# A last strip of 7 KB of each row instead of 6 KB, to release the first store sooner

## Chip, cores and metric

The kernel runs on one core of a Trainium2 chip. The metric is the device time of one execution in microseconds (us).

## The reference

```python
def setup_inputs():
    batch, c, h, w = 32, 3, 256, 256
    return {"x": np.random.randn(batch, c, h, w).astype(np.float32)}

def reference(x):
    return np.rot90(x, k=2, axes=(-2, -1)).astype(np.float32)
```

Each of the 96 images of 256 x 256 is turned by 180 degrees, that is, its 65,536 numbers are put in reverse order. 25.17 MB are read and 25.17 MB written.

## The kernel before

The input is cut into three tiles, A, Bt and Ct, each of 128 partitions with 64 KB (16,384 floats). VectorE reverses each row of a tile in place through a small tile T; the store writes the four rows of an image in reverse order. All transfers are issued by SyncE.

```python
    def load(t, g, lo, hi):
        return nc.sync.dma_start(out=t[:, lo:hi], in_=x4[g][:, lo:hi])

    def store(t, g):
        return nc.sync.dma_start(out=o4[g][:, ::-1, :], in_=t[:, :])
    # ... inside(t): 12 copies on VectorE that reverse a tile in place
    TAIL = 1536
    load(A, 0, 0, E)
    load(Bt, 1, 0, E)
    body = load(Ct, 2, 0, E - TAIL)
    load(Ct, 2, E - TAIL, E)
    inside(A)
    first = store(A, 0)
    tc.add_manual_dep(
        first.ins, body.ins.name,
        mybir.DependencyInfo(mybir.DependencyClass.Sync, mybir.DependencyReason.DATA),
        reason="the first store is queued while the last strip is on its way")
    for g, t in ((1, Bt), (2, Ct)):
        inside(t)
        store(t, g)
```

The third load is in two pieces, a body and a strip of `TAIL` columns. The first store doesn't need either; it is made to wait until the body has landed, and is issued while the strip is still on its way.

## Time and profile before

| | |
|---|---|
| median of 3 runs | 122.15 us (122.03 to 122.24) |
| DMA queue's share of 16 engines | 97.3% |
| VectorE busy | 37% |
| first store issued | 59.48 us |

The span of the profile (120.2 us) is shorter than the time: the rest lies outside the core's program. One more source is used below: the trace records the start and duration of every DMA packet. Every transfer shows 128 data packets, a row or a piece of a row in each, and 16 packets of 9 ns that count up the semaphore, one for each DMA engine; that is 8 rows and one semaphore packet for an engine. The records don't name the engine, so "the last strip end" is the latest end of such a packet over the 16 engines, "the mean strip end" their mean, and the same for the store's first packets. The "mean gap" is the mean start of the store's first packets less the mean strip end; the "bubble" is this idle time between strip and store. The "skew" is how far the last of the 16 semaphore packets of a transfer is behind their mean.

### The profile page before, as it was taken

To read this page: it belongs to the slowest core of one execution; us is meant where nothing else is said; L and a number is where in the kernel's file an instruction comes from. 1 tells how busy PE (TensorE), PEld (TensorE's weight loads), DVE (VectorE), ACT (ScalarE), POOL (GpSimd) and SP (SyncE) were. 2 spreads that over 40 slices of the span, in tenths; PEclk is the share of its full clock that TensorE was granted. 3 is DMA by queue.
4 is the path that set the end of the run, shared out by engine and by line. 5 is a ranking of instruction groups with operands and counts; after the bars stand their busy time and mean duration, and the time that the engine had idled before them with its cause. 6 is when DMAs were issued, how large, how long until landed. Compare 5 with 4: busy or idle time off the path is not lost.

```text
span 120.2 us, 93 instructions
## 1 busy us (share of the span) xinstructions
DVE 44.2 (37%) x36; POOL 0.2 (0%) x4
## 2 busy tenths in 40 slices
DVE  0000000499995099999059999400000000000000
POOL 0000000000000000000000000000000000000000
DMA  9888988898889779779499888988898889888990
GB/s 349 349 349 371 676 349 349 371 676 349 349 349 698 316 316 632 316 336 613 202 408 698 349 349 349 698 349 349 349 698 349 349 349 698 349 349 349 632 414 0
DMA packets 1008, 50.33 MB, mean 419 GB/s; under 512 B 112, under 2 KB 112, under 8 KB 240
## 3 DMA queue, kind: packets, MB, share of 16 engines
q1 hardware_dynamic: 1008, 50.33, 97.3%
HBM read 25.17 MB, written 25.17 MB: 419 GB/s over the span
## 4 chain that ended last, share of the span: by engine, by line
DMA 34%; DVE 25%; another core or an unknown queue 4%; issue 1%; SPq 0%; DVEq 0%
DMA Bt<-in_x_dram 34%; DVE T L52 8%; DVE Bt L52 8%; DVE Ct L52 8%; SPq L55 0%; DVEq L52 0%
## 5 line engine op out<-in xcount | busy, mean ns | idle before, releaser
L52 DVE COPY T<-A 128x2048 f32<-128x2048 f32 x4 | 4.9, 1227 | 22.6 <-DMA A<-in_x_dram 22.5
L52 DVE COPY T<-Ct 128x2048 f32<-128x2048 f32 x4 | 4.9, 1227 | 4.5 <-DMA Ct<-in_x_dram 4.4
L52 DVE COPY T<-Bt 128x2048 f32<-128x2048 f32 x4 | 4.9, 1227 | 4.4 <-DMA Bt<-in_x_dram 4.3
L52 DVE COPY Bt<-T 128x2048 f32<-128x2048 f32 x4 | 4.9, 1227 | 0.1
L52 DVE COPY A<-T 128x2048 f32<-128x2048 f32 x4 | 4.9, 1227 | 0.1
L52 DVE COPY Ct<-T 128x2048 f32<-128x2048 f32 x4 | 4.9, 1227 | 0.1
L52 DVE COPY A<-A 128x2048 f32<-128x2048 f32 x4 | 4.9, 1227 | 0.1
L52 DVE COPY Bt<-Bt 128x2048 f32<-128x2048 f32 x4 | 4.9, 1227 | 0.1
L52 DVE COPY Ct<-Ct 128x2048 f32<-128x2048 f32 x4 | 4.9, 1226 | 0.1
L95 POOL MEMSET const-uint8-127<- 128x1 uint8 x1 | 0.1, 102 | 0.0
L95 POOL MEMSET const-bfloat16-1.0<- 128x1 bf16 x1 | 0.1, 101 | 0.0
L95 POOL MEMSET const-float32-0.0<- 128x1 f32 x1 | 0.1, 98 | 0.2 <-issue 0.2
L95 POOL MEMSET const-float32-1.0<- 128x1 f32 x1 | 0.1, 98 | 0.0
## 6 DMA issues: line engine op xcount, KB each, us to landing
Ct<-in_x_dram SPq DMA_DIRECT2D x1, 7424.0 KB, 57.7
Ct<-in_x_dram SPq DMA_DIRECT2D x1, 768.0 KB, 59.2
A<-in_x_dram SPq DMA_DIRECT2D x1, 21.8
Bt<-in_x_dram SPq DMA_DIRECT2D x1, 40.7
out_dram<-A SPq DMA_DIRECT2D x1, 21.3
out_dram<-Bt SPq DMA_DIRECT2D x1, 39.9
out_dram<-Ct SPq DMA_DIRECT2D x1, 42.9
```

Source lines behind the costliest of these rows:

```text
L52: tc.keep_in_program_order(nc.vector.tensor_copy(out=dst, in_=src))
L95: nc = _bacc.Bacc("TRN2", target_bir_lowering=False, num_devices=1)
```

## The change

The intent is to let the first store be queued a little sooner, so that no DMA engine runs dry between the last load and the first store.

```diff
-    TAIL = 1536
+    TAIL = 1792
     load(A, 0, 0, E)
     load(Bt, 1, 0, E)
     body = load(Ct, 2, 0, E - TAIL)
```

## The prediction

> **What bounds the kernel now.** I read the page first: how busy each engine is, and what the DMA queue took.
>
> ```profile
> span 120.2 us, 93 instructions
> DVE 44.2 (37%) x36; POOL 0.2 (0%) x4
> ...
> q1 hardware_dynamic: 1008, 50.33, 97.3%
> HBM read 25.17 MB, written 25.17 MB: 419 GB/s over the span
> ```
>
> VectorE is busy for 37% of the span, the 16 DMA engines for 97.3%. All seven transfers are on one queue, so the kernel is one long row of packets per DMA engine: 24 rows of 64 KB in, 24 rows out. The reader should see how little is left: 2.7% of 120.2 us is 3.2 us, and the start (1.8 us before the first packet) and the end (1.1 us after the last one) hold 2.9 us of it. What lies between is some 0.3 us at most, and the change can only win part of that.
>
> Next the timeline and the waits of the DMA-issuing queue, to see what releases the stores.
>
> ```profile
> 1.64 1.01 SPq L55 DMA_DIRECT2D Ct<-in_x_dram  x2
> ...
> 36.39 1.23 DVE L52 COPY A<-T 128x2048 f32<-128x2048 f32 x1
> ...
> 59.48 0.63 SPq L58 DMA_DIRECT2D out_dram<-A  x1
> 60.20 0.55 SPq L58 DMA_DIRECT2D out_dram<-Bt  x1
> ...
> 76.51 0.54 SPq L58 DMA_DIRECT2D out_dram<-Ct  x1
> ```
>
> ```profile
> SPq L58 <- DMA Ct<-in_x_dram: 57.3, 2, 56.7
> ```
>
> A has been rotated since 37.6 us, but its store is issued only at 59.48, when the body of the third load has landed (its last semaphore increment is at 59.38): that is the added dependency. Only then does SyncE spend 0.63 us on the issue. The second store follows at 60.20, and the third at 76.51; the engines reach the second at about 80.2 and the third at about 99.5 (the packets with the stores' semaphore increments), so these two are never late, the third by 23 us.
>
> The page's chain of waits doesn't help here. It ends at VectorE's last copy (76.5 us) and calls 4.2 us "another core or an unknown queue": that is the landing of the third load. The end of the kernel is the end of the packets, so I looked at the packets alone, in the DMA view of the one microsecond from 60.10 to 61.10, in 40 slices of 25 ns, each packet counted where it starts:
>
> ```profile
> GB/s 737 737 737 246 246 492 246 246 246 492 737 246 246 246 737 0 492 246 0 0 492 0 0 0 0 0 7865 5243 7864 7865 2621 2621 5243 2621 0 0 0 0 0 0
> DMA packets 64, 1.25 MB, mean 1245 GB/s; under 512 B 16, under 2 KB 16, under 8 KB 48
> ```
>
> A 6 KB packet of the strip in a slice is 246 GB/s, a 64 KB packet of the store 2621. So the last two strip packets start in slice 20 (60.60 to 60.63), no packet starts in slices 21 to 25, and the 16 first store packets, one for each DMA engine, start in slices 26 to 33 (60.75 to 60.95). The packet records give the times behind it:
> - the strip's semaphore packets, the last on each engine: from 60.33 to 60.84 us, mean 60.644; each takes 9 ns;
> - the store's first packets: from 60.76 to 60.94 us, mean 60.833.
>
> The mean gap is 60.833 - 60.653 = 0.18 us on each engine. The records don't name the engine, but this mean needs no pairing. Between the first and second load the first packet follows within 10 ns of the semaphore packet (21.593, then 21.599): a full queue has no gap. So the 0.18 us is a bubble that the late release leaves.
>
> **What the Trainium skill says.** "DMA: Bandwidth & Descriptors", section "Queues, rings and completion order": on each engine, descriptors are consumed in ring order, on a ring that all DMAs of one issuing sequencer share. The trace agrees: semaphore packets of the seven transfers come in order of issue. So a store that is queued early waits behind the strip and doesn't overtake it. The same page, section "Why a DMA increments its semaphore by 16 and not by 1": only the full 16 means that all has landed. So the release is set by the body's slowest engine (its semaphore packet is at 58.99 us, its landing 0.39 later), while most engines finish earlier. The same page, "Latency and other measured facts", gives HWDGE about 600 ns to the first byte; here the first store packet starts 60.76 - (59.48 + 0.63) = 0.65 us after the issue ends, so it agrees. Its section "Where 436 GB/s comes from" puts the ceiling of this path at 435 GB/s; 65,536 B in 2.418 us, the usual packet here, are 27.1 GB/s on each engine and 434 on 16. No packet can be hoped to become quicker.
>
> **The change, part by part.** It removes nothing and adds nothing: the same seven transfers, copies and packets. The instruction order differs only in the shapes of the two pieces of the third load (14,848 and 1,536 columns become 14,592 and 1,792).
>
> Cost of the packets: a body packet of 59,392 B follows the next after 2.188 us and a strip packet of 6,144 B after 0.231, together 2.419, as a whole row of 64 KB takes (2.414 to 2.418). The fixed part is about 4 ns a packet. A row cut at 58,368 and 7,168 B is again two packets, so the strip ends where it ends now: cost 0.00 us.
>
> Move of the release: each engine carries 8 rows of the strip. Another 1,024 B of each is 8,192 B, at 27.1 GB/s 0.302 us. The body lands 0.30 us sooner, at about 59.08; the first store is issued at about 59.18 and could start its packets at 60.46 to 60.64 instead of 60.76 to 60.94.
>
> What of it reaches the end: an engine can start the store only when its strip is done, between 60.34 and 60.85. From its slowest body engine to its first store packet the release takes 60.762 - 58.991 = 1.77 us, to the last one 1.95; the strip now covers 8 x 0.231 = 1.85 of it, then 2.15. So the bubble closes on nearly all engines, and the strip becomes what they wait for. The mean start moves by 0.17 to 0.18 us. But the kernel ends with its last engine. The latest store start is 60.944 now and can't come before 60.851, the end of the last strip: 0.093 us. The three latest starts (60.900, 60.905, 60.944) against the three latest strip ends (60.771, 60.842, 60.851) give 0.13, 0.06 and 0.09. From there to the end an engine has 24 packets of 2.42 us whatever happens (the last semaphore packet, 119.104, is 58.16 after the latest start). So I expect 0.09 us from the bubble. To this may come 0.06 us: the store's first packets take 2.48 us, later ones 2.42; if that is the cost of starting an idle engine, it goes too. I count half: 0.03. Sum: about 0.12 us, 0.1% of 122.15, so 122.03.
>
> **The rivals.**
> - The whole 0.30 us reaches the end, which would be 121.85. For it: the release is moved by just that. Against it: the strip can't be hurried, and 0.18 is the mean gap.
> - Nothing reaches the end, 122.15. For it: the engine that ends last may be one whose gap is already nearly nil (the latest start and the latest strip end leave 0.09 at most if they belong to one engine; another engine may decide). The runs of the kernel before lie 0.21 us apart, so this looks the same as my own case in three runs.
> - Reads and writes run together and disturb each other, as the store starts on the quick engines while the slow ones still read their strips: up to 0.4 us of mixing instead of 0.08. If packets became 10% longer in that stretch, it would cost 0.04 us; 122.1. Against it: first store packets start at 60.76 already with strip packets running, and are 3% long.
> - The strip is held up by store packets that go ahead of it, and the third tile lands later. Harmless up to 23 us, as worked out above; the time stays at 122.0 to 122.15.
> - Longer body rows were better for the queue than shorter ones: excluded by the packet times above.
>
> **The range and the chances.** Every way above ends between 121.85 and 122.2; the scatter of the kernel before is 122.03 to 122.24. I predict 122.03 us, 8 in 10 between 121.82 and 122.23. A gain of 2% would be 2.4 us, eight times what all idle time between first and last packet amounts to; a loss of 2% would need a mechanism that nothing in the profile hints at. Faster by over 2%: 0.005. Within 2%: 0.985. Slower by over 2%: 0.01.
>
> **What would show it right or wrong.** In the changed profile: the first store issued at 59.1 to 59.25 instead of 59.48 (the release); its first packets starting between 60.45 and 60.86, more spread than now, with no empty stretch between strip and store (the bubble); the strip's semaphore packets still at 60.33 to 60.84 (no cost of the cut); VectorE's first copy of the third tile still near 61.4; the last packet at about 119.0 instead of 119.1. I am wrong if the store's first packets still start as one group later than the last strip packet, if strip or store packets get longer than 0.27 and 2.5 us, or if the end moves by over 0.3 us either way.

## The result, and the profile after

The changed kernel took 122.31 us (median of 6 runs, 122.04 to 122.44), the kernel before 122.20 us in 6 runs (122.03 to 122.77), 3 of them taken beside those of the changed kernel. The ratio is 0.9997, with a 95% interval from 0.9973 to 1.0021: no difference is seen. The predicted ratio was 0.999, inside the interval. As a time, 122.31 lies 0.08 us above the upper end of the predicted range.

The page of the changed kernel:

```profile
span 120.7 us, 93 instructions
DVE 44.2 (37%) x36; POOL 0.2 (0%) x4
...
q1 hardware_dynamic: 1008, 50.33, 97.2%
```

and its timeline around the release (start, duration, engine, instruction, and what ended the engine's wait):

```profile
59.63 0.63 SPq L58 DMA_DIRECT2D out_dram<-A  x1
60.36 0.55 SPq L58 DMA_DIRECT2D out_dram<-Bt  x1
61.82 1.23 DVE L52 COPY T<-Ct 128x2048 f32<-128x2048 f32 x1 [4.71 <-DMA Ct<-in_x_dram]
```

The first store is issued at 59.63 us, later than the 59.48 of before, though the body is shorter. This profiled run is the slowest of the six (122.44). The DMA view from 60.10 to 61.10 us in slices of 25 ns, as it was shown of before (a strip packet is now 287 GB/s, a store packet still 2621):

```profile
GB/s 573 287 573 860 287 287 860 573 0 0 287 573 287 860 860 0 0 860 287 0 0 0 574 0 287 287 0 0 287 0 0 0 10772 5243 5243 3195 2621 2621 2621 287
DMA packets 62, 1.06 MB, mean 1059 GB/s; under 512 B 12, under 2 KB 12, under 8 KB 50
```

Strip packets still start in slices 22 to 39 (the 287 in the last slice is one), and only 12 of the 16 semaphore packets are in the window: four engines are late. So the packet records, averaged over the 16 engines, say more:

| | before | after |
|---|---|---|
| body: semaphore packets, mean and last | 58.79, 58.99 | 58.70, 59.20 |
| strip end, mean and last | 60.65, 60.85 | 60.86, 61.36 |
| first store packets, first and last | 60.76, 60.94 | 60.91, 61.39 |
| mean gap from strip to store | 0.18 | 0.19 |
| last store start to last semaphore packet | 58.16 | 58.15 |

The mean engine did end its body sooner, but the slowest engine was 0.51 us behind the mean, against 0.20 before, and the release waits for the slowest. Seven body packets that started between 43 and 49 us took 2.26 to 2.46 us where 2.15 is usual, long before the release. The kernel before has such packets too: in its second profile (see below) four were over 5% long, up to 2.36 us where 2.19 is usual. So nothing says that the shorter body rows are at fault. So one profile of each kernel could not answer the question. It took a second profile of both, and larger steps of the same change.

### The profile page after: what moved, and what is told of

Same layout as the page of the kernel before. It is cut to its first block, busy times and chain, and to the rows that moved or that the text cites. A ratio compares the mean times of both kernels' runs of the same rounds, so it can differ in the third digit from the quotient of the medians.

```text
span 120.7 us, 93 instructions
## 1 busy us (share of the span) xinstructions
DVE 44.2 (37%) x36; POOL 0.2 (0%) x4
## 4 chain that ended last, share of the span: by engine, by line
DMA 34%; DVE 25%; another core or an unknown queue 4%; issue 1%; SPq 0%; DVEq 0%
DMA Bt<-in_x_dram 34%; DVE T L52 8%; DVE Bt L52 8%; DVE Ct L52 8%; SPq L55 0%; DVEq L52 0%
```

## The experiments

I began with the theory of the prediction (the "bubble" theory): the kernel ends when the slowest DMA engine's strip is done, plus what of the release's latency the strip doesn't cover, plus 58.16 us. Its rivals: the release is hidden by something else (A), reads and writes that overlap cost time (B), all time by which the release moves reaches the end (C). All ran on one chip.

### Shorter strips: 2 KB and 4 KB

```diff
-    TAIL = 1536
+    TAIL = 512      # e1_strip2k; 1024 in e2_strip4k
```

> Strip of 2 KB a row (512 columns) instead of 6 KB. My theory: the end is the strip end of the slowest DMA engine, plus whatever of the release's latency (1.77 to 1.95 us from the body's last semaphore packet to the store's first packets) the strip does not cover, plus 58.16 us of stores. The strip now covers 8 x 0.080 = 0.64 us instead of 1.85, so the bubble grows by 1.21 us on the slowest engine and the time by about 1.2 us, to 123.4 (ratio 1.010); the mean gap between strip and store rises from 0.18 to about 1.4 us. Rival A, the release is hidden anyway by something else: no change (122.2). Rival B, reads and writes that overlap cost time: less overlap, so less than the 1.2 us.

> Strip of 4 KB a row (1024 columns). My theory: the strip covers 8 x 0.155 = 1.24 us instead of 1.85, so the time rises by 0.60 us to about 122.8 (ratio 1.005), mean gap about 0.8 us. Rival A: 122.2. A straight line through 2, 4 and 6 KB with 0.30 us for each KB is what my theory says; the line must bend at 6 to 7 KB.

Measured: 2 KB: 122.71 us, ratio 1.0036 (1.0021 to 1.0051). 4 KB: 123.00 us, ratio 1.0063 (1.0048 to 1.0078), close to the expected 1.005. But the shorter strip being the quicker of the two fits no theory. The timeline of SyncE in the 2 KB run shows why:

```profile
57.22 0.63 SPq L58 DMA_DIRECT2D out_dram<-Bt  x1
61.31 0.55 SPq L58 DMA_DIRECT2D out_dram<-A  x1
77.18 0.54 SPq L58 DMA_DIRECT2D out_dram<-Ct  x1
```

The scheduler had put Bt's store first, which waits for no part of the third load. With 4 KB the mean gap was -0.003 us (with 2 KB the semaphore packets of body and strip overlap in time and can't be told apart, but a store packet starts within 10 ns of a semaphore packet there too). So there was no bubble to test, and a different loss: the strip's packets ran long, 12 of 128 by over 5% with 2 KB and 39 with 4 KB. These two runs say nothing about the bubble, and the near hit of 4 KB was luck.

### The 2 KB strip in the right order

```diff
-    TAIL = 1536
+    TAIL = 512
...
-        store(t, g)
+        last = store(t, g)
+        if g == 1:
+            tc.add_manual_dep(
+                last.ins, first.ins.name,
+                mybir.DependencyInfo(mybir.DependencyClass.NoSync, mybir.DependencyReason.DATA),
+                reason="the second store is queued after the first")
```

> The 2 KB strip again, now with the first store kept ahead of the second on the queue (in the two runs before, with 2 and 4 KB, the scheduler had put the second store first, so that a store was queued 2.7 to 3.5 us before the strip's end, and they did not test the bubble). Theory of the bubble: nothing is queued before the body has landed, strip 0.64 us, so the bubble grows by 1.21 us on the slowest engine, ratio 1.008 to 1.011, mean gap about 1.4 us, and no strip packet longer than 0.1 us. If the release is hidden: ratio 1.000.

Measured: 123.41 us, ratio 1.0096 (1.0079 to 1.0113), 1.17 us more (0.96% of 122.26) against the 1.21 worked out. The mean gap was 1.45 us, the last store start came 1.20 us after the last strip end instead of 0.08 to 0.09, and no strip packet took over 0.084. In the DMA view from 60 to 63 us (slices of 75 ns) the bubble can be seen as the zeros between strip and store:

```profile
GB/s 82 219 328 328 410 410 437 355 301 273 164 55 27 27 27 0 0 0 0 0 0 0 0 0 0 0 0 0 0 6117 6117 1748 0 0 0 0 0 0 0 0
```

So where the strip is too short, the missing cover does reach the end, nearly one to one. Rival A falls.

### Longer strips, or no dependency

```diff
-    TAIL = 1536
+    TAIL = 4096     # e3_strip16k
```
```diff
-    first = store(A, 0)
-    tc.add_manual_dep(first.ins, body.ins.name, ...)
+    store(A, 0)     # e4_nodep
```

> Strip of 16 KB a row (4096 columns): the release comes 3.0 us sooner than with 6 KB, far ahead of the strip's end on every engine. My theory: no gap on any engine (mean under 0.03 us), end earlier by the 0.06 to 0.1 us that the slowest engine's gap had, so 122.0 to 122.2 (ratio 0.999, not to be told from 1). Rival C, all released time reaches the end: ratio 0.975. Rival B, mixing of reads and writes costs: packets longer than 2.42 us around 58 to 64 us and ratio over 1.002.

> The added dependency is taken away; the first store is queued when its tile is rotated, at 37.6 us, the second at 57, while the loads still have 20 us to go. My theory (ring order, a full queue has no gap): as the 16 KB strip, no gap on any engine, ratio 0.998 to 1.001. Rival B (queued stores disturb the loads, which would be why the dependency was put in): load packets longer from 38 us on, and slower by tenths of a us or more.

Measured: 16 KB: 123.07 us, ratio 1.0061 (1.0045 to 1.0078). Without the dependency: 123.14 us, ratio 1.0074 (1.0059 to 1.0089). The gaps are gone (in the 16 KB run the store's first packet starts 3 ns before the recorded end of the semaphore packet, on every engine in order of time), and the kernel is 0.8 to 0.9 us slower. My theory missed this. Of rival B, which the prediction had put at 0.04 us, the loss came true, but not all of the mechanism: the packets of the body and of the store were as short as ever (2.20 and 2.418 us without the dependency). Only the strip's packets got long: without the dependency they took 0.395 us on average and up to 0.935, where the kernel before has 0.234. Eight of them cost an engine 8 x (0.395 - 0.234) = 1.29 us. The store phase gives 0.2 us back: from the last store start, 57.95 us to the end instead of 58.16, in the 16 KB run.

### Which store slows the strip

Without the dependency two stores are queued before the strip ends, at 37.9 and at 57.3 us. This run queues only the first early:

```diff
-    load(Ct, 2, E - TAIL, E)
+    strip = load(Ct, 2, E - TAIL, E)
...
-    first = store(A, 0)
-    tc.add_manual_dep(first.ins, body.ins.name, ...)
+    store(A, 0)
...
-        store(t, g)
+        last = store(t, g)
+        if g == 1:      # the store of Bt waits for the strip
+            tc.add_manual_dep(last.ins, strip.ins.name, ...)
```

> As without the dependency, but only the first store is queued early (37.6 us); the second waits until the strip has landed. It tells apart what slows the strip from 58.6 us on: the second store's issue at 57.3 us (then the strip runs at full speed here, ratio 0.998 to 1.000) or the first store waiting behind the strip in the same rings (then the same long packets from about 58.6 us on, and ratio about 1.007 as without the dependency). I expect the second, 70 to 30.

Measured: 123.06 us, ratio 1.0066 (1.0051 to 1.0082); strip packets 0.377 us on average, up to 0.973. So the first store alone is enough. Its issue at 37.7 us did no harm for 20 us: body packets took 2.20 us on average, as in the kernel before (2.19). Only the strip, the last packets ahead of it, ran slow. In the DMA view from 58 to 62 us (slices of 100 ns, a 6 KB packet is 61), the kernel before:

```profile
GB/s 0 0 0 0 61 61 61 369 307 553 369 369 492 369 492 369 553 307 492 492 184 614 307 430 307 184 123 3277 5243 1966 0 0 0 0 0 0 0 0 0 0
```

and with the first store queued early:

```profile
GB/s 0 0 0 0 0 123 61 123 184 369 430 246 184 246 0 307 246 246 123 123 61 246 0 369 123 184 123 184 123 246 492 307 369 430 369 1085 1024 1557 3400 2028
```

Both strips begin at about 58.5 us. Before, some 400 GB/s of packets start in each slice and the last at 60.6; here it is around 200 GB/s up to 61.0, recovers, and the store begins from 61.5 on.

### Where the loss begins: 8, 10 and 12 KB

```diff
-    TAIL = 1536
+    TAIL = 2048     # e6_strip8k; 2560 in e7_strip10k, 3072 in e9_strip12k
```

> Strip of 8 KB a row. The store's packets are ready 0.60 us sooner than with 6 KB, so on the mean engine some 0.4 us before its strip ends. Theory M (a store that is queued behind a strip slows the strip's packets, as with 16 KB and without the dependency, where they took 2 to 4 times as long; the loss grows with the overlap): strip packets lengthened on some engines, mean end of the strip later by up to 0.2 us, and ratio 0.999 to 1.002. Theory of the bubble alone: ratio 0.998 to 0.9995, no long packets, mean gap under 0.05 us.

> Strip of 10 KB a row: packets ready 1.2 us sooner than with 6 KB, 0.8 to 1.2 us before the strip's end. Theory M: a loss between that of 8 and of 16 KB, ratio 1.002 to 1.005, and the long packets begin about 1.3 us after the store's issue. Theory of the bubble alone: as 8 KB, ratio 0.998 to 0.9995.

> Strip of 12 KB a row: store ready 1.8 us sooner than with 6 KB, 1.4 to 1.8 us before the strip's end. Theory M (a queued store slows the strip behind which it waits): between 10 KB (0.9995, hardly any long packets) and 16 KB (1.006, packets up to 2.2 times as long): ratio 1.001 to 1.005, long strip packets from about 1.3 us after the store's issue. If instead only the 16 KB packets themselves were at fault: no long packets, ratio 0.999.

Measured: 8 KB: 122.11 us, ratio 0.9990 (0.9975 to 1.0005), no long strip packet. 10 KB: 122.15 us, 0.9995 (0.9976 to 1.0013), 11 of 128 strip packets over 5% longer than usual. 12 KB: 122.49 us, 1.0021 (1.0004 to 1.0039), 14 of 128, up to 0.852 us instead of 0.460. With 16 KB it was 45 of 128. So a loss is seen from 12 KB on, where the interval is just clear of 1, and it is larger with 16 KB. Not as expected was the time of the long packets: the issues are at 58.54 (10 KB) and 58.08 us (12 KB), the store can be ready 1.28 us later, and most long packets start before that, around the issue itself. Those can't be put down to a store that is ready and waits; packets lengthened by 0.1 to 0.3 us show up in the middle of the load phase without any store queued (the seven at 43 to 49 us above). With 16 KB they begin where expected, at 58.09, which is 1.3 us after the issue at 56.77. So theory M is supported by the runs with the store queued well ahead, and not shown for 10 and 12 KB.

### Both kernels again, and 8 KB

The changed kernel, the kernel before and the 8 KB strip ran once more, unedited (for the third: `TAIL = 2048`), with 5 rounds each.

> The changed kernel (7 KB strip) once more. Bubble theory: the gain on the slowest DMA engine is 0.06 to 0.1 us, so a ratio of 0.9985 to 1.0005 against before. In the profile: store issued 1.27 to 1.5 us before its first packet, and a mean gap between 0.06 and 0.19 us, smaller where the 16 engines end the body within 0.6 us of each other, larger where some engine lags, because the release waits for the slowest and the others wait with it.

> The kernel before against itself, for the noise and for a second profile. Ratio 1.000 within 0.001. In the profile: the mean gap again near 0.18 us or larger with a larger skew, the last store start to the last semaphore packet again 58.15 to 58.2 us, and the end of the loads on the slowest engine anywhere between 60.8 and 61.4 us: if it differs from the first profile by 0.2 us or more, the drift of the load phase alone is larger than the whole expected gain.

> Strip of 8 KB a row once more, timed longer, as the best candidate: its mean gap was 0.08 us and its ratio 0.999 with an interval over 1. Expected 0.998 to 1.0000; gap under 0.1 us; no long strip packets.

Measured: changed kernel 122.22 us, ratio 1.0006 (0.9987 to 1.0026); kernel before against itself 122.25 us, 0.9997 (0.9985 to 1.0010); 8 KB 122.16 us, 0.9993 (0.9981 to 1.0004). The release and the DMA view from 60.10 to 61.10 us (25 ns slices) of the second profile of the changed kernel:

```profile
59.29 0.63 SPq L58 DMA_DIRECT2D out_dram<-A  x1
```

```profile
GB/s 573 573 287 860 287 287 0 573 573 287 0 573 573 573 287 0 0 287 2908 7865 287 2622 5243 2622 287 5243 0 2621 2622 2622 0 5243 0 0 0 0 0 0 2621 0
DMA packets 58, 1.24 MB, mean 1235 GB/s; under 512 B 16, under 2 KB 16, under 8 KB 42
```

and of the second profile of the kernel before:

```profile
GB/s 737 492 492 246 492 246 492 246 492 492 246 737 0 492 246 492 246 246 737 0 246 0 246 246 246 0 0 0 0 0 0 246 0 0 0 0 0 13107 5243 7864
DMA packets 62, 0.88 MB, mean 883 GB/s; under 512 B 15, under 2 KB 15, under 8 KB 52
```

In the changed kernel store packets (2621 and more) start from slice 18 on while strip packets (287) still start in slices 20 and 24: the empty stretch is gone. The 16th store packet, alone in slice 38, is the engine that comes last. In the kernel before, slices 25 to 36 hold a single strip packet, and the stores start together from slice 37 on. The packet records of the six profiles (us):

| profile | body: last behind mean | mean gap | last strip end | last store start | their difference |
|---|---|---|---|---|---|
| before, 1st | 0.20 | 0.18 | 60.851 | 60.944 | 0.093 |
| before, 2nd | 0.39 | 0.35 | 61.138 | 61.217 | 0.079 |
| 7 KB, 1st | 0.51 | 0.19 | 61.363 | 61.388 | 0.025 |
| 7 KB, 2nd | 0.31 | 0.06 | 60.979 | 61.066 | 0.087 |
| 8 KB, 1st | 0.46 | 0.08 | 61.091 | 61.162 | 0.071 |
| 8 KB, 2nd | 0.26 | 0.06 | 60.952 | 61.044 | 0.092 |

The mean gap shrinks with the longer strip, and it follows the skew of the 16 engines (the second column), because all wait for a release that the slowest sets. The last column hardly changes: 0.079 and 0.093 us before, 0.025 to 0.092 with longer strips. With 7 and 8 KB a single store packet starts after the last strip end, so there it is the slowest engine's own gap; before, five and three start after it, so there it is only the most that this engine's gap can be. And the last strip end, which the change doesn't move, differs by 0.29 us between two profiles of the same kernel before.

## Why the prediction was right or wrong

**What bounds the kernel** was right. In each of the six profiles of the table the last store start plus 58.15 to 58.17 us is the last semaphore packet. VectorE's last copy ends more than 20 us before the engines reach its tile's store. The 2 KB strip in the right order showed the bubble term with the size that the prediction's arithmetic gives (1.17 us against 1.21). One citation of the prediction is shortened: the section "Where 436 GB/s comes from" gives 435 GB/s for the SBUF ports, and says of transfers between HBM and SBUF that a lower limit, about 358 GB/s, binds. This trace, with one core at work, shows 434.

**The release** moved as worked out, but only relative to the slowest engine. It was to come at 59.18 us and came at 59.63 and 59.29, because that engine's body ended at 59.20 and 58.82 instead of the 58.69 that follows from the first profile and the 0.30 us. The prediction took one profile's skew of the engines as fixed.

**The mean bubble** was to close from 0.18 us to almost nothing. It was 0.19 and 0.06, against 0.18 and 0.35 before: nearly closed in the second profile, where the skew was 0.31 us, and not in the first, where it was 0.51. With 8 KB it was 0.08 and 0.06, so the smaller gap isn't one profile's luck.

**The step that failed** is "the latest store start is 60.944 now and can't come before 60.851 ...: 0.093 us", taken as a gain. The bound was right, but the slowest engine didn't reach it: it kept a gap of 0.025 and 0.087 us with 7 KB, although the store was ready. The last store start less the last strip end so fell from 0.086 us on average to 0.056, by 0.03 instead of 0.09, and the two profiles of each kernel lie too far apart to call even this a gain. In the second profile the first store packet of any engine starts at 60.57 us, while the last engine's strip ends at 60.98. A lead of 0.4 us, from when the store could start to the end of the strip, didn't close its gap.

In the 10 KB run, where the store is ready at about 58.54 + 1.28 = 59.82 and the last strip ends at 61.25, the gap of this last engine, with a lead of 1.4 us, was gone (-0.003). The first engine of the same run, with a lead of 0.66 us, still had a gap of 0.08 us or more (its strip ends at 60.48, and no store packet starts before 60.56). With 12 KB all leads are about 1.3 us or more, and no engine has a gap. So a lead of up to 0.7 us wasn't enough and 1.3 us was; why, the runs don't say.

So the bubble closed on the quick engines, which then finish early (their last semaphore packets spread over 0.54 us in the second profile instead of 0.21), and the end is where it was. By the prediction's own sign ("if the end moves by over 0.3 us") the first profile speaks against it: the packets end at 119.55 us instead of 119.11. But the strip's end had moved by 0.51 us, and the kernel before ended at 119.40 in its second profile: the load phase drifts by more than the sign allows for.

**The 0.03 us for warm first packets** was mis-sized as well: they took 2.472 and 2.461 us with 7 KB on average, against 2.477 and 2.476 before. They come down to 2.418 in the 12 and 16 KB runs, where the queue is full in good time. There the whole store phase is 0.2 us shorter (57.95 us from the last store start to the end), so more was at stake than the 0.06 us of the first packets; with 7 KB the last engine won none of it (58.15 and 58.17).

**The total**, 0.12 us or a ratio of 0.999, can't be told from none: the ratios 0.9997 and 1.0006 have intervals of 0.2% to each side, twice the predicted gain. No gain was shown, and the packet records show 0.03 us on average for the last engine, which two profiles of each kernel can't tell from none. The absolute 122.03 was too low for another reason too: the kernel before itself measured 122.20 and 122.25 in later rounds.

**The rivals.** "Nothing reaches the end" is the nearest by the numbers. Its reason, that the engine that ends last has nearly no gap to lose, isn't settled: the profiles before leave this engine a gap anywhere from 0.00 to 0.09 us. "The whole 0.30 us" would be a ratio of 0.9975; the second interval excludes it (from 0.9987 on), the first by itself doesn't (from 0.9973 on), and with 8 KB it would be 0.995, which both intervals exclude. Mixing of reads and writes was dismissed with a cost of 0.04 us. For 7 KB that stands: one strip packet of 256 in two profiles was over 5% longer than usual. What a store costs that is queued well ahead was underrated: 0.6 to 0.7%, which the dependency of the kernel before saves. The prediction took from ring order that such a store "waits behind the strip and doesn't overtake it". The starts did keep this order (without the dependency, each first store packet starts as a strip's semaphore packet ends), but the strip ahead ran slow all the same. The section cited adds that data descriptors carry no barrier, so that a later one may finish its write first; no run here shows that. What exactly slows the strip isn't settled: that reads and writes disturb each other is argued and not tested by itself.

No version was shown to be quicker than both kernels. The 8 KB strip had 0.9990 and 0.9993, with intervals up to 1.0005 and 1.0004.

## What to carry to other kernels

Where 16 DMA engines finish a transfer at different times, a release waits for the slowest one and the kernel ends with the slowest one, so closing the mean gap between two phases can gain less than its length (here 0.29 us of mean gap closed from one second profile to the other, and no gain in time was seen); look at the last engine's gap, and take two profiles before trusting a tenth of a microsecond. A store that is queued long before the loads ahead of it are done wasn't free here: between too late (a bubble, seen at 2 KB) and too early (slower loads, seen from 12 KB on) lies a stretch, 6 to 10 KB, in which no difference was seen, and a change of 1 KB inside it shows nothing. When a dependency is moved, check that the scheduler kept the order of the transfers.

## What the Trainium skill lacked or had wrong

- "DMA: Bandwidth & Descriptors", section "Rules for kernel authors", advises to issue a DMA early and wait late. It doesn't say that a store queued behind loads can slow them: issued at 37.7 us instead of 59.5, the first store lengthened the 6 KB strip packets from 0.234 to 0.377 us on average and cost 0.66% of the time.
- The same page, section "Two DMAs through the same engine are not ordered", says that descriptors of one queue start in order but are pipelined, with separate queues for the read and write sides of an engine. That leaves room for a store's reads to run beside the strip, but the page gives no cost, and no run here shows the read side by itself.
- No page gives the skew of the 16 engines at the end of a transfer: the body's last semaphore packet was 0.20 to 0.51 us behind the mean engine's in the six profiles of the table.
- No page says how far ahead a store must be queued for the engines to pass from loads to stores without loss: with the store ready 0.4 to 0.7 us before the end of its strip, the slowest engine kept a gap of 0.03 to 0.09 us (7 and 8 KB) and took 58.15 to 58.17 us to the end; with about 1.3 us or more (12 KB) no engine had a gap, and it took 57.95.
